# Narrower causal score products, one softmax scale taken out to the head's norm, and one Strassen product added up in PSUM

## The chip, the cores and the metric

The kernel runs on one core of one Trainium2 chip. The metric is the device time of one execution in microseconds; the figure for a kernel is the median of its runs. One more execution is recorded with the hardware profiler: it gives the profile page and the trace from which all rows below come. In them PE is TensorE (matmuls and transposes), PEld its weight loads, DVE is VectorE, ACT is ScalarE, POOL is GpSimd, and SP is the queue that issues most DMAs.

## The reference

One decoder layer over 1024 tokens and 1024 channels, in fp32: RMSNorm; a projection to differential attention (4 heads of two components, dimension 64 each, values 128 wide), sliding-window attention and two gates; a gated merge and a residual; RMSNorm; a gated MLP with a causal convolution of width 3; a residual; a last RMSNorm. The parts that the change touches:

```python
# differential attention, per block of 128 queries
s = einsum(q_blk, k) * scale
logits = where(dist >= 0, s - slopes * dist, NEG_INF)
p = softmax(logits)
a = p[:, :, 0] - lam * p[:, :, 1]
o = einsum(a, v)
o = rmsnorm(o, subln_w) * (1.0 - lam_init)      # over the head's 128 channels, eps 1e-6
...
x = x + (silu(gate) * val) @ w_down             # D_FF = 2816 = 22 blocks of 128
```

## The kernel before

Activations lie with channels on the partitions, so a product of a 128 x 128 weight tile with 512 tokens is one matmul into one PSUM bank. Every fp32 operand is split into a high part (rounded for TensorE, a cast on ScalarE, tiles `wh`, `sh`, `h`) and a low part (a subtraction on VectorE, tiles `wl`, `sl`, the second half of `h`), and a product takes three matmuls: high by high, high by low, low by high. The large products use a seven-product (Strassen-Winograd) scheme on 2 x 2 blocks; the sums of weight blocks that it needs are made by GpSimd in `sum_pair` (L86), which loads a pair of weight tiles `g` and `v`, and are split by `split_pair` (L104).

A tile framework orders the instructions of each engine by priorities and by its own estimates, and sets the waits; each engine, and each DMA queue, then runs its own list strictly in order. Buffers are taken from pools by tag, a fixed number for each; a new tile waits until the last reader of the one whose place it takes is done.

**Attention.** For each head u (4 of them) and each block i of 128 queries, `da_step` (L553) makes the scores of both components against keys 0 to (i+1)*128, rounded up to 256 columns, in cuts of at most 512 (L566, two matmuls for each cut, for the two parts of the keys). VectorE adds the bias and takes the row's extreme (L570), ScalarE takes the exponential and its row sum (L571), VectorE the reciprocal (L572); the second component's is multiplied by -lambda (L574) and applied by ScalarE (L577), and L578 combines both. Transposes to PSUM (L584), a split (L586, L587), and `da_av` (L591) for the product with the values follow. `da_norm` (L601) makes the head's RMSNorm out of column sums on PE (L159), a power -1/2 on GpSimd (`rstd_cols`, L168) and a spread of the result by PE transposes (L174); it is spread over the first steps of the next head. Half-products of the gate projection (`back_half`, L151 to L153, tile `g`) stand between the attention steps and fill PE.

**Down projection.** `down` (L968) treats the 22 blocks of the hidden width in three ranges. Blocks 0 to 5 are plain products in 16 pieces (`self.pieces`, made in `plan`): an output block m (of 8) and a half c (three blocks each); each piece is 2 halves of the tokens by 3 blocks by 3 matmuls, L1016. A bank `pss[m, hf]` holds the sum of both c, and after c = 1 VectorE adds it to the residual `x3` (L1034). `pss[m, 0]` are banks of tag "d", `pss[m, 1]` of tag "y", four of each. In these pieces the h tiles for the later ranges are loaded (`hr`), cast (L748) and made low (L749), and the sums of h blocks for the Strassen part are formed (`sums_h`, L930). Blocks 6 to 13 are the Strassen part. A first loop over m = 0 to 3 makes A11 B11 into a "y" bank and A12 B21 into a "d" bank (`product`, L828 to L830) and adds both to x3 (L1044); a second loop makes the other five products. Blocks 14 to 21 are plain products and the last norm.

Weights for all this come through `next_w` and `ahead` in the order of `self.wsrc`, into three raw buffers (tag "raw"). The pair of weight tiles for the sums of m = 0 (kind "sums") stands before the last two loads of the pieces, and takes two of the three raw buffers until GpSimd's four sums (L97 to L100) are done.

Of the kernel before, what the change touches and what calls it, by code (L numbers as in the profile page):

```python
# [43 lines left out]
class Trunk:  # L44
# [23 lines left out]
    def ahead(self, n):  # L68
        while len(self.wq) < n and self.wsrc and (self.wsrc[0][1] != "pair" or self.uw):
            src, nk, *eng = self.wsrc.pop(0)  # L70
            if nk == "sums":

                self.sums = self.split_pair(*self.sum_pair(src, True), 1, 3)
            elif nk == "rest":
                self.sums["A22"] = self.load_w(src[1][:, 4:8], 4)
                self.wq.append(self.sums)
            elif nk == "pair":
                first, skip = eng or (False, 0)
                self.wq.append(self.split_pair(*self.sum_pair(src, first), skip))
            else:  # L80
                self.wq.append(self.load_w(src, nk, *eng))
        if self.deep and self.wsrc and len(self.wsrc[0]) == 2 and not isinstance(self.wsrc[0][1], str):

            src, nk = self.wsrc[0]
            self.wsrc[0] = src, nk, None, None, self.load_raw(src, nk)

    def sum_pair(self, src, first=False):


        nc = self.nc  # L90
        g = self.tl(self.wp, [P, 2, 4, P], "raw", bufs=RAW)
        nc.sync.dma_start(g.rearrange("p a k c -> p (a k) c"), src[0])
        v = self.tl(self.wp, [P, 2, 4, P], "raw", bufs=RAW) if first else self.tl(self.uw, [P, 2, 4, P], "rv", bufs=2)
        nc.sync.dma_start(v.rearrange("p a k c -> p (a k) c"), src[1])
        sa, sb = (self.tl(self.sfp[0], [P, 2, 4, P], self.sfp[1]) for _ in range(2))
        tt = nc.gpsimd.tensor_tensor
        tt(sa[:, 0], v[:, 0], v[:, 1], ALU.add)  # L97
        tt(sa[:, 1], sa[:, 0], g[:, 0], ALU.subtract)  # L98
        tt(sb[:, 0], g[:, 0], v[:, 0], ALU.subtract)  # L99
        tt(sb[:, 1], g[:, 1], sa[:, 1], ALU.subtract)  # L100
        return g, v, sa, sb
# [116 lines left out]
    def plan(self):  # L218

        self.kind = {m: "q" if m < 4 or 12 <= m < 16 else "k" if m < 8 or m == 16 else "v" if m < 18 else "g" for m in range(34)}  # L220


        self.plain = [0, 4, 8, 18, 20]
        self.pairs = [(1, 5), (9, 2), (6, 10), (3, 7), (11, 12), (13, 16), (17, 14), (15, 19)]
        gates = list(range(21, 34))
        self.back = []
        todo = [(m, hf) for m in gates for hf in range(2)]
        for steps in HALVES:
            self.back.append([[todo.pop(0) for _ in range(n)] for n in steps])
        assert not todo  # L230
        src = [(self.w_in[m], KC) for m in self.plain]
        src += [((self.w_in[a], self.w_in[b]), "pair") for a, b in self.pairs]
        src += [(self.w_in[m], KC) for m in gates]
        src += [(self.w_br[m], KC) for m in range(KC)]
        self.mix_order = [m for k in range(4) for m in (k, k + 4)]
        src += [(self.w_mix[m], KC) for m in self.mix_order]
        src += [((self.w_up[j], self.w_up[j + NF]), "pair") for j in range(NF)]


        n, n2 = N1 // 2, NF - N1 - 8  # L240
        self.pieces = [(m, c) for m0 in (0, 4) for c in range(2) for m in range(m0, m0 + 4)]
        src += [(self.w_dn[m:m + 2, :, n * c:n * c + n, :].rearrange("m p k c -> p m k c"), 2 * n) for m, c in self.pieces[::2]]
        pairs = [(self.w_dn[m, :, N1:N1 + 8, :], self.w_dn[m + 4, :, N1:N1 + 8, :]) for m in range(4)]
        src.insert(len(src) - 2, (pairs[0], "sums"))
        src += [(self.w_dn[m, :, N1:N1 + 8, :], 8) for m in range(4)]
        src += [(pairs[0], "rest")] + [(p, "pair", True, 1) for p in pairs[1:]]
        src += [(self.w_dn[m, :, N1 + 8:, :], n2) for _ in range(2) for m in range(KC)]
        self.wsrc, self.wq, self.deep = src, [], False
# [175 lines left out]
    def attention(self):  # L424
        nc, tc = self.nc, self.tc
        with ExitStack() as ctx:
# [27 lines left out]
            for u in range(6):  # L454
                if st is None:
                    st = self.q_stacks(u), self.kv_stacks(u)
                if u < 4:
                    self.v_parts(u)
                elif u == 4:
                    self.sw_v(self.v32(17))  # L460
                y = self.tl(self.fpool, [P, T], "y", bufs=2) if u < 4 else None
                aT = None
                for i in range(NB):
                    if u < 4:
                        if i % 2 == 0:
                            aT = self.da_at(i // 2)
                        self.da_step(u, i, st, aT)
                        if i % 2 == 1:
                            self.da_av(u, i // 2, aT, y)
                    else:  # L470
                        self.sw_step(u - 4, i, st)
                    for b in self.back[u + 1][i]:
                        self.back_half(*b)
                    self.flush(1)
                    if later:
                        later.pop(0)()
                st = None
                if u < 4:
                    later = self.da_norm(u, y)
# [73 lines left out]
    def da_step(self, h, i, st, aT):  # L553
# [1 line left out]
        q, k = st  # L555
        slope = 4.0 ** -(h + 1)
        w = (i + 1) * P
        wp = (w + 255) // 256 * 256
        pr, rr = [], []
        for c in range(2):  # L560
            sc = self.tl(self.psS, [P, T], "sc")
            qs = q[c][:, i * P:(i + 1) * P]
            for part in range(2):
                for n0 in range(0, wp, H2):
                    n1 = min(n0 + H2, wp)
                    nc.tensor.matmul(sc[:, n0:n1], qs, k[c][part][:, n0:n1], start=part == 0, stop=part == 1)  # L566
            L = self.tl(ap, [P, T], "L", bufs=4)
            s = self.tl(self.st, [P, 4], "sm", bufs=8)
            o = 896 - i * P
            nc.vector.tensor_tensor_reduce(L[:, :w], sc[:, :w], self.bias[:, o:o + w], slope, 3e38, ALU.add, ALU.min, s[:, 0:1])  # L570
            nc.scalar.activation(L[:, :w], L[:, :w], AF.Exp, bias=s[:, 0:1], scale=-1.0, accum_out=s[:, 1:2])  # L571
            nc.vector.reciprocal(s[:, 2:3], s[:, 1:2])  # L572
            if c == 1:
                nc.vector.tensor_tensor(s[:, 2:3], s[:, 2:3], self.neglam, ALU.mult)  # L574
            pr.append(L)
            rr.append(s[:, 2:3])
        nc.scalar.mul(pr[1][:, :w], pr[1][:, :w], rr[1])  # L577
        nc.vector.scalar_tensor_tensor(pr[0][:, :w], pr[0][:, :w], rr[0], pr[1][:, :w], ALU.mult, ALU.add)  # L578
        qo = (i % 2) * P
        for j0 in range(0, i + 1, 4):  # L580
            nj = min(4, i + 1 - j0)
# [19 lines left out]
    def da_norm(self, h, y):  # L601

        nc, ap = self.nc, self.ap
        sqs = []
        for hf in range(2):
            sqs.append(self.tl(ap, [P, H2], "sq", bufs=1))
            nc.scalar.activation(sqs[hf], y[:, hf * H2:(hf + 1) * H2], AF.Square)
# [4 lines left out]

        def sums():
            self.col_sums(ssq, sqs[1:], 4, 4)
            box.append(self.rstd_cols(ssq, 8, P))

        def half(hf):
            ps = self.tl(self.psT, [P, H2], "t")
# [349 lines left out]
    def down(self):  # L968

        nc, tc = self.nc, self.tc  # L970
        with ExitStack() as ctx:
# [31 lines left out]
            for i, (m, c) in enumerate(self.pieces):  # L1003
# [5 lines left out]
                for hf in range(2):  # L1009
                    if c == 0:  # L1010
                        pss[m, hf] = bank(hf)
                    js = range(n * c, n * c + n)
                    for q, j in enumerate(js):
                        h, l = self.hs[hf, j]
                        for p, (v, x) in enumerate(((w[0], h), (w[0], l), (w[1], h))):
                            nc.tensor.matmul(pss[m, hf], v[:, q, :], x, start=c == q == p == 0, stop=c == 1 and q == n - 1 and p == 2)  # L1016
                if i in (2, 8):
                    ms = slice(i // 8 * 4, i // 8 * 4 + 4)
                    nc.sync.dma_start(x3[:, ms], self.x2d[ms].rearrange("m p t -> p m t"))
                for _ in range(n if i < 2 else 1):  # L1020
                    if preps:
# [7 lines left out]
                if i == len(self.pieces) - 1:  # L1029
                    sums.pop(0)()  # L1030
                if c == 1:
                    for hf in range(2):
                        x = col(m, hf)
                        tt(x, x, pss[m, hf], ALU.add)  # L1034
            assert not preps
            ys = []
            for m in range(4):
                wh, wl = self.next_w()
                y, ps = bank(1), bank(0)
                ys.append(y)  # L1040
                self.product(y, (wh[:, 0:4], wl[:, 0:4]), "B11", skip=True)
                self.product(ps, (wh[:, 4:8], wl[:, 4:8]), "B21")
                for p in (y, ps):
                    tt(col(m, 0), col(m, 0), p, ALU.add)  # L1044
                if sums:
                    sums.pop(0)()
# [156 lines left out]
```

## Time and profile before

| | |
|---|---|
| median of 3 runs | 1358.22 us (1357.28 to 1360.21) |
| the profiled execution | 1359.85 us, its span 1358.0 us |
| granted TensorE clock, mean | 0.997 |
| PE busy | 1337.9 us (99% of the span), 6316 matmuls |
| VectorE, ScalarE, GpSimd busy | 1009.0, 623.3, 464.7 us |

A matmul's duration in the trace contains the way through the array, which overlaps with the next one's: where PE is dense, the spacing of starts is what a matmul costs. Rows of the timeline give start, length, engine, line, operation, the tiles written and read, shapes and count; in brackets stands the idle time before it and what ended it. Rows of groups give count, busy time in us, mean duration in ns, and idle time before them. Rows of the view of waits give in total, times, longest.

### The profile page before, as it was taken

Reading aid. Unit: us, or ns where it says so; the run is one execution under the profiler, and the core shown is the slowest. Engines: PE = TensorE matmul, PEld = TensorE weight load, DVE = VectorE, ACT = ScalarE, POOL = GpSimd, SP = SyncE. Lnnn points to the kernel's source line nnn. Section 1 sums busy time; section 2 is a strip of 40 time slices with the busy share of each in tenths; the row PEclk is TensorE's granted clock in tenths of the full one; section 3 lists DMA queues with packets and bytes.
Section 4 is the critical chain, followed back from the end, with each engine's and each line's share of the span. In section 5 each row is a group of like instructions: output and inputs, shape, how many; then the busy total and the mean of one; then the engine's idle time right before and its main releaser. Section 6 shows DMA issues by size and latency. Waiting matters only on the chain.

```text
span 1358.0 us, 17192 instructions
## 1 busy us (share of the span) xinstructions
PE 1337.9 (99%) x6316; PEld 1106.8 (82%) x6316; DVE 1009.0 (74%) x1485; ACT 623.3 (46%) x975; POOL 464.7 (34%) x326
## 2 busy tenths in 40 slices
PE   8999999999999999999999999999999999999997
PEld 6888888788888888888878888888888888788886
DVE  8746774688778966445689889888988898886454
ACT  9432232678776764344354333433343344333343
POOL 0436641000000015642455565556555611231011
PEclk9999999999999999999999999999999999999999
DMA  6334436755654246324522222222222248551342
GB/s 255 140 110 164 145 140 219 205 150 144 171 134 146 79 129 228 140 95 131 162 78 94 78 78 93 69 87 78 93 66 89 85 157 303 190 180 70 92 133 86
DMA packets 62757, 179.50 MB, mean 132 GB/s; under 512 B 6864, under 2 KB 15184, under 8 KB 62672
## 3 DMA queue, kind: packets, MB, share of 16 engines
q1 hardware_dynamic: 50640, 159.93, 36.5%
q10 hardware_dynamic: 12032, 18.46, 3.7%
q8 instruction: 50, 0.82, 0.3%
q14 instruction: 35, 0.29, 0.1%
HBM read 129.61 MB, written 48.76 MB: 131 GB/s over the span
## 4 chain that ended last, share of the span: by engine, by line
PE 61%; DVE 19%; issue 9%; POOL 5%; DMA 2%; ACT 2%; POOLq 0%; SPq 0%; DVEq 0%; ACTq 0%
POOL us L958 5%; PE g L151 5%; PE g L153 5%; PE g L152 5%; PE t L828 4%; PE t L830 4%; PE t L829 4%; PE y L989 3%; PE d L989 3%; PE sc L153 3%; PE sc L152 3%; PE sc L151 3%; DVE wl L113 3%; DVE c L951 3%; PE sc L566 3%
## 5 line engine op out<-in xcount | busy, mean ns | idle before, releaser
L963 ACT ACTIVATE c<-us,vecs 128x1024 f32<-128x1024 f32 x44 | 54.8, 1248 | 163.1 <-POOL us L958 159.6
L958 POOL TENSOR_TENSOR us<-us,rstd 128x1024 f32<-128x1024 f32 x42 | 100.3, 2407 | 53.9 <-DVE wl L132 35.6
L130 ACT CAST wh<-raw 128x1024 fp32r<-128x1024 f32 (+2 forms) x62 | 62.8, 1012 | 110.2 <-PE sc L152 34.9
L111 ACT CAST sh<-sf 128x1024 fp32r<-128x1024 f32 x60 | 62.8, 1050 | 101.3 <-POOL sf L98 62.4
L132 DVE TENSOR_TENSOR wl<-raw,wh 128x1024 fp32r<-128x1024 f32 (+2 forms) x62 | 84.7, 1366 | 31.8 <-ACT wh L130 31.2
L964 DVE SCALAR_TENSOR_TENSOR c<-us,vecs,c 128x1024 f32<-128x1024 f32 x44 | 66.3, 1509 | 51.2 <-ACT c L963 51.2
L97 POOL TENSOR_TENSOR sf<-rv 128x512 f32<-128x512 f32 x29 | 41.9, 1446 | 162.0 <-DMA rv<-in_w_up 63.5
L113 DVE TENSOR_TENSOR sl<-sf,sh 128x1024 fp32r<-128x1024 f32 x60 | 83.7, 1397 | 8.0 <-ACT sh L111 8.0
L718 POOL TENSOR_TENSOR gr<-gr,rstd 128x1024 f32<-128x1024 f32 x16 | 40.3, 2521 | 130.3 <-PE t L670 91.1
L151 PE MATMUL g<-xh,wh 128*128 128x512 f32 x208 | 83.5, 402 | 0.3 <-ACT g L496 0.3
L152 PE MATMUL g<-xl,wh 128*128 128x512 f32 x208 | 83.1, 400 | 0.0
L153 PE MATMUL g<-xh,wl 128*128 128x512 f32 x208 | 82.8, 398 | 0.0
L168 POOL TENSOR_TENSOR rs<-ms,mhalf 128x8 f32<-128x8 f32 (+2 forms) x9 | 14.5, 1609 | 169.6 <-DVE ms L166 163.6
L570 DVE CUSTOM_DVE_ANT_0 L<-sc,bias 128x128 f32<-128x128 f32 (+7 forms) x64 | 47.9, 752 | 22.4 <-PE sc L566 17.3
L99 POOL TENSOR_TENSOR sf<-raw,rv 128x512 f32<-128x512 f32 x29 | 40.4, 1391 | 58.7 <-DVE sl L113 58.7
L965 DVE SCALAR_TENSOR_TENSOR c<-us,vecs,c 128x1024 f32<-128x1024 f32 x44 | 57.2, 1301 | 0.6
L98 POOL TENSOR_TENSOR sf<-sf,raw 128x512 f32<-128x512 f32 x30 | 56.7, 1890 | 1.6
L550 POOL MEMSET aT<- 128x128 f32 x32 | 6.1, 206 | 145.5 <-PE t L597 99.6
L113 DVE TENSOR_TENSOR wl<-raw,wh 128x1024 fp32r<-128x1024 f32 (+1 forms) x34 | 52.5, 1545 | 0.1
L566 PE MATMUL sc<-u,u 128*128 128x512 f32 (+1 forms) x192 | 51.1, 371 | 1.4 <-issue 0.8
L571 ACT ACTIVATE L<-L,sm 128x128 f32<-128x128 f32 (+7 forms) x64 | 49.4, 776 | 6.3 <-DVE sm L570 5.3
L151 PE MATMUL sc<-mh,wh 128*128 128x512 f32 x128 | 49.8, 389 | 0.0
(437 smaller groups left out, 4317.6 us busy)
## 6 DMA issues: line engine op xcount, KB each, us to landing
u<-qd SPq DMA_DIRECT2D x72, 256.0 KB, 6.6
raw<-in_w_down SPq DMA_DIRECT2D x28, 512.0 KB, 3.7
raw<-in_w_in SPq DMA_DIRECT2D x26, 512.0 KB, 4.2
hr<-hd SPq DMA_DIRECT2D x50, 256.0 KB, 5.3
raw<-in_w_up SPq DMA_DIRECT2D x23, 512.0 KB, 3.5
hd<-c SPq DMA_DIRECT2D x22, 512.0 KB, 2.7
rv<-in_w_up SPq DMA_DIRECT2D x21, 512.0 KB, 3.5
gr<-gd SPq DMA_DIRECT2D x16, 512.0 KB, 3.4
```

Of the source, the lines that this page charges most:

```text
L111: nc.scalar.copy(hi, src)
L113: nc.vector.tensor_tensor(lo, src, hi.bitcast(F32), ALU.subtract)
L130: self.hi = nc.scalar.copy(wh, raw)
L132: self.lo = (eng or nc.vector).tensor_tensor(wl, raw, wh.bitcast(F32), ALU.subtract)
L151: nc.tensor.matmul(ps, wh[:, kc + o, :], ah, start=first and n == 0, stop=False)
L152: nc.tensor.matmul(ps, wh[:, kc + o, :], al, start=False, stop=False)
L153: nc.tensor.matmul(ps, wl[:, kc + o, :], ah, start=False, stop=last and n == len(kcs) - 1)
L566: nc.tensor.matmul(sc[:, n0:n1], qs, k[c][part][:, n0:n1], start=part == 0, stop=part == 1)
L958: i = (nc.vector if m % NF == 0 else nc.gpsimd).tensor_tensor(us[:, 2:], us[:, 2:], self.rstd, ALU.mult)
L964: nc.vector.scalar_tensor_tensor(c, us[:, 1:T + 1], cw[1], c, ALU.mult, ALU.add)
L965: nc.vector.scalar_tensor_tensor(c, us[:, 0:T], cw[0], c, ALU.mult, ALU.add)
L989: nc.tensor.matmul(ps, v[:, n, :], x, start=n == i == 0, stop=n == len(js) - 1 and i == 2)
```

## The change

Five edits.

- **Scores of used columns only.** Block i has w = (i+1)*128 keys. Before, the product covered w rounded up to 256. Now it covers w columns, but 256 at i = 0. At w = 640 the scores are laid 128 columns into their two PSUM banks, so that the cuts (384 and 256) fit a bank each.
- **First component's 1/sum in the norm.** With s0 and s1 the row sums of the two exponentials, the kernel now forms E0 - lambda (s0/s1) E1, which is s0 times what it formed before: the reciprocal of s1, then s0 times it times -lambda as one scalar operation, then one combining operation on VectorE. The multiplication on ScalarE and the first reciprocal go. The sums s0 of a head are kept in a 128 x 8 tile, and `da_norm` puts 1/s0 back: the column sums are multiplied by (1/s0) squared ahead of the power, and the result by 1/s0 behind it (on GpSimd).
- **A12 B21 in PSUM.** For m = 0 to 3, `pss[m, 0]` is kept, and A12 B21 of the first loop is added onto it by TensorE; one addition on VectorE then takes both to x3.
- **Order of the pieces.** Output blocks 4 to 7 come first, then 0 to 3; the two loads of x3 follow that.
- **Buffer of the pair's second tile.** For the kind "sums", `v` takes a buffer of tag "sl" of the down projection's pool in place of a raw buffer.

```diff
-                self.sums = self.split_pair(*self.sum_pair(src, True), 1, 3)
+                self.sums = self.split_pair(*self.sum_pair(src, True, "sl"), 1, 3)
...
-    def sum_pair(self, src, first=False):
+    def sum_pair(self, src, first=False, idle=None):
...
-        v = self.tl(self.wp, [P, 2, 4, P], "raw", bufs=RAW) if first else self.tl(self.uw, [P, 2, 4, P], "rv", bufs=2)
+        v = self.tl(self.wp, [P, 2, 4, P], "raw", bufs=RAW) if first and not idle else self.tl(self.uw, [P, 2, 4, P], idle or "rv", bufs=2)
...
-        self.pieces = [(m, c) for m0 in (0, 4) for c in range(2) for m in range(m0, m0 + 4)]
+        self.pieces = [(m, c) for m0 in (4, 0) for c in range(2) for m in range(m0, m0 + 4)]
...
-        wp = (w + 255) // 256 * 256
-        pr, rr = [], []
+        lo = P if w == 640 else 0
+        cuts = ((0, 256),) if i == 0 else ((0, w),) if w <= H2 else ((0, H2 - lo), (H2 - lo, w))
+        pr = []
...
-                for n0 in range(0, wp, H2):
-                    n1 = min(n0 + H2, wp)
-                    nc.tensor.matmul(sc[:, n0:n1], qs, k[c][part][:, n0:n1], start=part == 0, stop=part == 1)
+                for n0, n1 in cuts:
+                    nc.tensor.matmul(sc[:, lo + n0:lo + n1], qs, k[c][part][:, n0:n1], start=part == 0, stop=part == 1)
...
-            nc.scalar.activation(L[:, :w], L[:, :w], AF.Exp, bias=s[:, 0:1], scale=-1.0, accum_out=s[:, 1:2])
-            nc.vector.reciprocal(s[:, 2:3], s[:, 1:2])
-            if c == 1:
-                nc.vector.tensor_tensor(s[:, 2:3], s[:, 2:3], self.neglam, ALU.mult)
+            nc.scalar.activation(L[:, :w], L[:, :w], AF.Exp, bias=s[:, 0:1], scale=-1.0, accum_out=s[:, 1:2] if c else self.s0[:, i:i + 1])
             pr.append(L)
-            rr.append(s[:, 2:3])
-        nc.scalar.mul(pr[1][:, :w], pr[1][:, :w], rr[1])
-        nc.vector.scalar_tensor_tensor(pr[0][:, :w], pr[0][:, :w], rr[0], pr[1][:, :w], ALU.mult, ALU.add)
+
+        nc.vector.reciprocal(s[:, 2:3], s[:, 1:2])
+        nc.vector.tensor_scalar(s[:, 3:4], self.s0[:, i:i + 1], s[:, 2:3], self.neglam, ALU.mult, ALU.mult)
+        nc.vector.scalar_tensor_tensor(pr[0][:, :w], pr[1][:, :w], s[:, 3:4], pr[0][:, :w], ALU.mult, ALU.add)
...
-            box.append(self.rstd_cols(ssq, 8, P))
+            r0, t = (self.tl(self.st, [P, NB], n, bufs=2) for n in ("r0", "r2"))
+            nc.vector.reciprocal(r0, s0)
+            nc.vector.tensor_tensor(t, r0, r0, ALU.mult)
+            nc.vector.tensor_tensor(t, t, ssq[:, :NB], ALU.mult)
+            rs = self.rstd_cols(t, 8, P)
+            nc.gpsimd.tensor_tensor(rs, rs, r0, ALU.mult)
+            box.append(rs)
...
-                            nc.tensor.matmul(pss[m, hf], v[:, q, :], x, start=c == q == p == 0, stop=c == 1 and q == n - 1 and p == 2)
+                            nc.tensor.matmul(pss[m, hf], v[:, q, :], x, start=c == q == p == 0, stop=c == 1 and q == n - 1 and p == 2 and (m > 3 or hf > 0))
...
-                    ms = slice(i // 8 * 4, i // 8 * 4 + 4)
+                    ms = slice(4 - i // 8 * 4, 8 - i // 8 * 4)
...
-                    for hf in range(2):
+                    for hf in range(m < 4, 2):
                         x = col(m, hf)
                         tt(x, x, pss[m, hf], ALU.add)
...
-                y, ps = bank(1), bank(0)
+                y, ps = bank(1), pss[m, 0]
...
-                self.product(ps, (wh[:, 4:8], wl[:, 4:8]), "B21")
+                self.product(ps, (wh[:, 4:8], wl[:, 4:8]), "B21", first=False)
```

More of the change, by code (lines that the diff above doesn't have):

```diff
@@ L464, in attention @@
                     if u < 4:
+                        if i == 0:
+                            self.s0 = self.tl(self.st, [P, NB], 's0', bufs=2)
                         if i % 2 == 0:
@@ L569, in da_step @@
             o = 896 - i * P
-            nc.vector.tensor_tensor_reduce(L[:, :w], sc[:, :w], self.bias[:, o:o + w], slope, 3e38, ALU.add, ALU.min, s[:, 0:1])
-            nc.scalar.activation(L[:, :w], L[:, :w], AF.Exp, bias=s[:, 0:1], scale=-1.0, accum_out=s[:, 1:2])
-            nc.vector.reciprocal(s[:, 2:3], s[:, 1:2])
-            if c == 1:
-                nc.vector.tensor_tensor(s[:, 2:3], s[:, 2:3], self.neglam, ALU.mult)
+            nc.vector.tensor_tensor_reduce(L[:, :w], sc[:, lo:lo + w], self.bias[:, o:o + w], slope, 3e38, ALU.add, ALU.min, s[:, 0:1])
+            nc.scalar.activation(L[:, :w], L[:, :w], AF.Exp, bias=s[:, 0:1], scale=-1.0, accum_out=s[:, 1:2] if c else self.s0[:, i:i + 1])
             pr.append(L)
-            rr.append(s[:, 2:3])
-        nc.scalar.mul(pr[1][:, :w], pr[1][:, :w], rr[1])
-        nc.vector.scalar_tensor_tensor(pr[0][:, :w], pr[0][:, :w], rr[0], pr[1][:, :w], ALU.mult, ALU.add)
+        nc.vector.reciprocal(s[:, 2:3], s[:, 1:2])
+        nc.vector.tensor_scalar(s[:, 3:4], self.s0[:, i:i + 1], s[:, 2:3], self.neglam, ALU.mult, ALU.mult)
+        nc.vector.scalar_tensor_tensor(pr[0][:, :w], pr[1][:, :w], s[:, 3:4], pr[0][:, :w], ALU.mult, ALU.add)
         qo = (i % 2) * P
@@ L603, in da_norm @@
         nc, ap = self.nc, self.ap
-        sqs = []
+        sqs, s0 = [], self.s0
         for hf in range(2):
```

## Prediction, made before the changed kernel ran

> **What bounds the kernel now.** I read the page's first two parts, then the windows by stage, then the PE timeline wherever a window is short of full, and last the queues that feed that place.
>
> ```profile
> span 1358.0 us, 17192 instructions
> PE 1337.9 (99%) x6316; PEld 1106.8 (82%) x6316; DVE 1009.0 (74%) x1485; ACT 623.3 (46%) x975; POOL 464.7 (34%) x326
> ```
>
> ```profile
> 240.00:480.00 240.00, 238.73 (x1417) 1.00 0.52 144
> ...
> 1180.00:1200.00 20.00, 18.27 (x73) 0.91 0.65 215
> ```
>
> The windows' columns are stretch, length, PE busy (count), granted clock, DMA share, GB/s. TensorE has work 99% of the span; in attention (240 to 480 us) it is idle for 1.27 of 240 us. So time comes off in two ways only: columns that PE need not stream, or one of its few holes. The one hole that this change touches lies at 1180 to 1200, where PE is 1.73 us short and the clock falls to 0.91. Work taken from ScalarE or VectorE elsewhere buys nothing by itself.
>
> **The score products.** PE's pace is the spacing of starts, not a matmul's duration. The chain of waits gives it for 256 and for 512 columns, the PE timeline for 512-column scores among other attention work:
>
> ```profile
> 392.54 1.92 PE sc L650 x16
> 1257.75 5.44 PE d L989 x24
> ```
>
> ```profile
> 264.08 0.86 PE L566 MATMUL sc<-u,u 128*128 128x512 f32 x3
> 264.79 0.27 PE L597 MATMUL t<-aT,v 128*128 128x256 f32 x1
> ```
>
> 256 columns cost 1.92/16 = 0.120 us, 512 cost 5.44/24 = 0.227, and in attention (264.79 - 264.08)/3 = 0.237. The new cuts leave i = 0, 1, 3, 5 and 7 alone; at i = 2, 4 and 6 one 512-wide product becomes 384 wide: 3 steps x 2 components x 2 parts x 4 heads = 48 matmuls. No row shows 384 columns. On the line between 256 and 512 it takes 0.227 - 0.107/2 = 0.1735 us, 0.0535 less, so 48 x 0.0535 = **2.6 us**, all on PE's path. (With 0.237, 2.8.) The bounds: as dear as 512 columns, 0; as cheap as 256, 48 x 0.107 = 5.1. I take the line, because each of the 48 sits between two measured widths of the same instruction. It could also be dearer than 512: 128-column transposes start 0.109 us apart,
>
> ```profile
> 266.56 0.71 PE L584 MATMUL t<-ident,L 128*128 128x128 f32 x5
> 267.02 0.48 PE L151 MATMUL g<-xh,wh 128*128 128x512 f32 x1
> ```
>
> where five start within 0.46 us, the last spaced short. At 0.109 per 128 columns, 384 would cost 0.327, or 48 x 0.100 = 4.8 us more than now; I give that little weight, since those are plain fp32 transposes.
>
> The Trainium skill, TensorE: Matmul & The Clock Gate, section Back-to-back issue gap, says that in a stream of weight load and matmul the spacing is set by both, 81 ns at 128 columns and 131 at 512. By that slope 128 columns are worth 17 ns and the edit 0.8 us. The trace disagrees with the level (0.227 at 512), and its own slope between 256 and 512 is the one used above.
>
> **Softmax and norm.** Off ScalarE go 32 multiplications, off VectorE 32 reciprocals; a scalar product takes the place of the one with -lambda.
>
> ```profile
> L577 ACT ACTIVATE L<-L,sm 128x128 f32<-128x128 f32 (+7 forms) x32 | 24.3, 775 | 2.7 <-DVE sm L574 2.3 <-DVE sm L572 0.3
> L572 DVE RECIPROCAL sm<-sm 128x1 f32<-128x1 f32 x64 | 9.6, 157 | 6.2 <-ACT L L571 6.0
> ```
>
> That is 24.3 us of ScalarE and 5.0 of VectorE, beside a PE that idles 1.27 us in the whole stage, with gate products between the softmax steps. I book 0. The order of the changed program has the same attention work on PE, with fewer gate matmuls between some steps, so a wait may come or go; I bound it at 1.3 gained (all idle) and 2 lost. Each head's norm gets a reciprocal and two 128x8 products on VectorE (0.16 each, like L572) and one 128x8 product on GpSimd, ahead of the transposes at L174:
>
> ```profile
> 287.98 1.65 POOL L168 TENSOR_TENSOR rs<-ms,mhalf 128x8 f32<-128x8 f32 x1 [3.24 <-DVE sm L572]
> ```
>
> ```profile
> 293.35 0.60 PE L174 MATMUL t<-ident,rs 128*128 128x128 f32 x4
> ```
>
> rs is ready at 289.63, its reader starts at 293.35: 3.7 us of cover. At worst the GpSimd product costs as much as this power, 1.65, and VectorE 0.3 behind the sums. It stays hidden; without cover it would be 4 x 2 = 8 us.
>
> **The down projection's hole.** PE's rows there:
>
> ```profile
> 1182.72 0.39 PE L830 MATMUL d<-h,wl 128*128 128x512 f32 x1
> 1184.23 0.50 PE L828 MATMUL y<-h,wh 128*128 128x512 f32 x1 [1.12 <-ACT wh L130]
> 1184.56 0.40 PE L829 MATMUL y<-h,wh 128*128 128x512 f32 x1
> 1185.57 0.50 PE L830 MATMUL y<-h,wl 128*128 128x512 f32 x1 [0.61 <-DVE wl L132]
> ...
> 1186.75 0.63 PE L828 MATMUL y<-h,wh 128*128 128x512 f32 x1
> ...
> 1189.74 0.43 PE L829 MATMUL d<-h,wh 128*128 128x512 f32 x1
> 1190.01 0.39 PE L830 MATMUL d<-h,wl 128*128 128x512 f32 x1
> ```
>
> From 1182.72 to 1190.01 there are 15 steps (the rows left out counted), 3.40 us at 0.227; it takes 7.29. The hole costs **3.89 us**: 1.28 and 0.78 waiting for the second weight tile (m = 1) of the A11 / A12 loop, and the rest, 1.83, mostly because the seven spacings from 1186.75 to 1189.74 are 0.427, nearly half pace. Why it was late:
>
> ```profile
> ACT h L748 <- DVE hr L936: 6.4, 1, 6.4
> ```
>
> ```profile
> 1170.01 1.23 DVE L113 TENSOR_TENSOR sl<-c,sh 128x1024 fp32r<-128x1024 f32 x1 [2.27 <-ACT sh L111]
> 1171.15 0.68 DVE L1034 TENSOR_TENSOR x<-x,d 128x512 f32<-128x512 f32 x1
> ...
> 1183.70 0.68 DVE L1034 TENSOR_TENSOR x<-x,y 128x512 f32<-128x512 f32 x1
> 1184.30 1.21 DVE L132 TENSOR_TENSOR wl<-raw,wh 128x1024 fp32r<-128x1024 f32 x1
> ```
>
> VectorE works without a pause from 1171.15, 21 operations deep (an add lets the next start after 0.60 us, a low part like sl after 1.14), before that tile's low part, and ScalarE's cast of the high part stands behind two h casts that wait for VectorE. The change takes four of the adds away (A12 B21 lands in the same bank) and moves others: in the changed program's order 14 operations stand there, 13 of 0.60 and one low part of 1.14.
>
> Against this the pair's second tile v goes to a "sl" buffer whose memory still holds parts of hidden tiles; its load now waits for PE's last use of them, in piece 11 (before, it had a raw buffer that came free earlier), and the casts of the sums stand ahead of the first A11 weight on ScalarE. Worked forward:
>
> ```profile
> 1159.60 0.39 PE L1016 MATMUL y<-sl,wl 128*128 128x512 f32 x1
> ```
>
> ```profile
> 1163.07 1.62 POOL L98 TENSOR_TENSOR c<-c,raw 128x512 f32<-128x512 f32 x1
> 1164.66 2.00 POOL L99 TENSOR_TENSOR c<-raw,raw 128x512 f32<-128x512 f32 x1
> 1166.62 2.27 POOL L100 TENSOR_TENSOR c<-raw,c 128x512 f32<-128x512 f32 x1
> ```
>
> ```profile
> 1160.06 9.67 SPq L120 DMA_DIRECT2D raw<-in_w_down  x4
> ```
>
> ```profile
> raw<-in_w_down SPq DMA_DIRECT2D x28, 512.0 KB, 3.7
> ```
>
> ```profile
> 1168.92 1.05 ACT L111 CAST sh<-c 128x1024 fp32r<-128x1024 f32 x1 [3.14 <-POOL c L100]
> ```
>
> ```profile
> 1177.51 0.39 PE L828 MATMUL y<-h,wh 128*128 128x512 f32 x1
> ```
>
> PE lets v's place go at 1159.99; the load of the first A11 weight leaves SP ahead of it, at 1160.06, so v leaves about 1160.5 and lands at 1164.2. GpSimd's four sums: three take 5.82 here, with a first like L98 7.4, so 1171.6. The sh cast ends at 1172.7, its low part (1.23) at 1173.9, and 14 operations later (13 x 0.60 + 1.14) VectorE starts the m = 1 low part at 1182.8, done at 1184.0. PE starts m = 0 at 1177.51 (its own low part is done at 1175.7, needed at 1177.96), m = 1 24 x 0.227 later at 1182.96, and needs that low part at 1183.41: late by 0.6. With v landing in 3.2 to 4.9 us and sums of 6.1 to 7.4 it is on time or late by up to 1.7. I book 0.7 left, with no half pace, so **3.2 us** gained (2.2 with 1.7 left and full pace; 0.4 if the 1.83 of half pace stay too; 3.9 at most). Queued behind v on SP are the m = 1 and m = 2 weights, wanted 20 us later, and h loads for the same sums. x3's two loads trade halves, at the same places.
>
> The Trainium skill, TensorE: Matmul & The Clock Gate, Part 1 (the HAM clock gate), has half clock after an idle window of some 3.4 us. Here two waits of 2.06 us together, within 2.6, were enough; by the page the half pace would not be there at all, and the hole worth 2.06. The measurement decides.
>
> **The sum.** 2.6 + 0 + 3.2 = 5.8 us. The profiled execution took 1359.85 us (its span 1358.0 and 1.9 around it), so 1354.05 for its like. It stood 1.63 above the median of the three runs, 1358.22; on the level of that median I predict 1352.4.
>
> **Rivals.**
> 1. The forecast, with the score saving on the line and the hole nearly shut: 1350.5 to 1354.5 by itself. Chance 0.55.
> 2. The hole stays half open: late by 1.7, and the clock falls again. Then 2.6 + 0.4 = 3.0, 1355.2. For it: ScalarE and VectorE now wait for the sums ahead of the A11 weights. Against: 7 fewer operations in the queue. 0.16.
> 3. The 384-wide product costs what 512 costs, so that part doesn't do what it says: 3.2 gained by the hole alone, 1355.0. For it: each matmul has its own weight load (6316 of each). Against: 256 columns do run at 0.120. 0.09.
> 4. More than forecast: the softmax chain, shorter by a ScalarE multiplication of 0.78, closes attention's idle time, and the hole shuts fully: 2.8 + 1.3 + 3.9 = 8.0, 1350.2 or below. 0.08.
> 5. Slower: v lands late. If it takes 6.6 us, as the stacks' loads do, and the sums 9.65 (1159.24 to 1168.89, the waiting first one included), the low part of the sums ends at 1179.0 instead of 1173.9. Then m = 0 waits to 1180.8 instead of 1177.96 (2.8), m = 1 another 2.9, and each pays 1.8 of half pace: 9.3 against 3.9. Net 5.4 - 2.6 = 2.8 slower, 1361.0. It decides from an end of the sums' low part 4 us past 1173.3. For it: rows as long exist.
>
> ```profile
> u<-qd SPq DMA_DIRECT2D x72, 256.0 KB, 6.6
> 1159.24 3.75 POOL L97 TENSOR_TENSOR c<-raw 128x512 f32<-128x512 f32 x1 [6.56 <-DVE c L951]
> ```
>
> Against: loads of this very source take 3.7. With dearer 384-wide products (1361.0 if both gains were lost to them) 0.12.
>
> **How the numbers follow.** About 0.2%, 2.7 us, is what a measurement here can tell from no change. Faster by more than that, below 1355.5: cases 1 and 4 and half of 2 and 3 (1355.0 and 1355.2 lie near the edge), 0.75. Within: the other half and mild forms of 5, 0.15. Slower: 0.10. The range takes case 4 at its low end, 1349.0, and on the high end cases 2 and 3 together (0.4 left of gain, 1357.8): 1349.0 to 1357.8.
>
> **What would show it.** 48 score rows of 384 columns spaced 0.17; L577's row gone with PE's idle in attention as before, within 1 to 2 us; the window after the down pieces at clock 1.00 with at most one wait, under 1 us, at the second A11 weight; v's load near 1160 of the old clock. Wrong, if PE waits over 2 us there, if spacings of 0.43 return, or if attention has grown.

## The result, and the profile after

The changed kernel takes 1362.24 us (median of 8 runs, 1361.71 to 1363.84) where the kernel before takes 1358.40 in the same comparison (8 runs, 1356.93 to 1360.21): a ratio of 1.003, 95% interval 1.0019 to 1.0041. It is slower, by some 4 us, where 6 us of gain were forecast. The profiled execution took 1363.84 us.

The first lines of the changed kernel's page, and its windows for attention and for the place of the hole in the down-projection (columns as in the prediction, with PE, PEld, DVE, ACT and POOL in turn):

```profile
span 1362.1 us, 17126 instructions
...
PE 1344.8 (99%) x6316; PEld 1108.5 (81%) x6316; DVE 1014.3 (74%) x1461; ACT 604.3 (44%) x943; POOL 464.2 (34%) x330
```

```profile
240.00:480.00 240.00, 238.40 (x1429) 204.49 (x1428) 195.08 (x596) 156.48 (x400) 12.68 (x35) 1.00 0.53 147
1180.00:1200.00 20.00, 19.53 (x87) 15.85 (x86) 18.01 (x27) 7.01 (x10) 0.00 (x0) 1.00 0.69 225
```

Both places that the change edits are better. The hole is down from 1.73 us to 0.47 and the clock is full, and ScalarE is relieved by 19 us. PE is nevertheless busy 6.9 us longer with the same 6316 matmuls, 48 of which became narrower. A busy time that grows with less to stream says that matmuls have become slower. Where the time went, the starts of PE's matmuls show; the five columns run from the start of the trace to the last matmul:

| us | up to the first gate product | attention | merge and mix | hidden stage | down-projection and end |
|---|---|---|---|---|---|
| before | 219.8 | 289.4 | 173.8 | 429.2 | 239.6 |
| after | 223.7 | 286.4 | 174.8 | 432.5 | 238.5 |

Attention won 3.0 us and the down-projection 1.1. What was lost stands in three stages of which the change does not touch a line: 3.9, 1.0 and 3.3 us. The groups of PE's matmuls between 60 and 200 us, before and after (columns: count, then busy us and mean ns of one):

```profile
L828 PE MATMUL t<-xh,wh 128*128 128x512 f32 x56 | 21.8, 389 | 0.0
L829 PE MATMUL t<-xl,wh 128*128 128x512 f32 x56 | 21.8, 389 | 0.0
L830 PE MATMUL t<-xh,wl 128*128 128x512 f32 x56 | 21.8, 389 | 0.0
```

```profile
L835 PE MATMUL t<-xh,wh 128*128 128x512 f32 x56 | 22.1, 394 | 0.0
...
L837 PE MATMUL t<-xh,wl 128*128 128x512 f32 x56 | 22.0, 392 | 0.0
...
L836 PE MATMUL t<-xl,wh 128*128 128x512 f32 x56 | 21.7, 388 | 0.0
```

The three lines that are L828 to L830 before are L835 to L837 after. Their matmuls last 5, 3 and -1 ns longer, and the windows of 140 us, PE full and the clock at 1.00 in both, hold 619 matmuls before and 613 after:

```profile
60.00:200.00 140.00, 140.00 (x619) 115.99 (x618) 90.03 (x88) 41.07 (x48) 72.67 (x41) 1.00 0.41 147
```

```profile
60.00:200.00 140.00, 140.00 (x613) 114.89 (x612) 91.97 (x87) 40.93 (x48) 71.90 (x40) 1.00 0.43 153
```

In spacings that is 231.7, 229.2 and 225.8 ns for the three rows after, in their order, where all were 226 to 227. Added up over all 512-wide matmuls of the trace that are spaced under 260 ns, pace above 226.7 ns costs 3.4 us before and 15.9 after. 8.6 us of the latter lie in the hidden stage, where what spacings over 260 ns (mostly waits) add shrank from 6.8 to 2.3 us: a slower PE probably finds more of its operands ready.

The stage after attention holds the clue. In the merge and the mix, lines L151 to L153 run the same shapes; three groups between 512 and 685 us before, and six after:

```profile
L151 PE MATMUL sc<-mh,wh 128*128 128x512 f32 x128 | 49.8, 389 | 0.0
L152 PE MATMUL sc<-ml,wh 128*128 128x512 f32 x128 | 49.8, 389 | 0.0
L153 PE MATMUL sc<-mh,wl 128*128 128x512 f32 x128 | 49.8, 389 | 0.0
```

```profile
L151 PE MATMUL sc<-mh,wh 128*128 128x512 f32 x128 | 50.4, 394 | 0.0
L153 PE MATMUL sc<-mh,wl 128*128 128x512 f32 x128 | 50.2, 392 | 0.0
L152 PE MATMUL sc<-ml,wh 128*128 128x512 f32 x128 | 49.7, 388 | 0.0
L151 PE MATMUL g<-yh,wh 128*128 128x512 f32 x64 | 24.9, 389 | 0.0
L152 PE MATMUL g<-yl,wh 128*128 128x512 f32 x64 | 24.9, 389 | 0.0
L153 PE MATMUL g<-yh,wl 128*128 128x512 f32 x64 | 24.9, 389 | 0.0
```

After, the groups with `mh` and `ml` as the moving operand (the one that is streamed past the weights) have changed, those with `yh` and `yl` have 389 ns as before. In the built kernel the three tiles that the norm's edit adds to the pool `st` (`s0`, `r0`, `r2`: two buffers of 32 bytes per partition each, 192 in all) push up by 192 bytes every pool that is allocated after it from the left end of SBUF (the on-chip memory that both operands are read from): `raw` from 9216 to 9408, `wh` from 21504 to 21696. Pools allocated from the right end stay (`xh0` at 163328). Before, both operands of every 512-wide matmul begin at a multiple of 256 bytes. After, `wh`, `yh` and `yl` are 192 off and `mh`, `ml` and `xh` 0 off: in this stage slow where weight and moving operand differ, at pace where they agree. In the hidden stage the rule does not hold matmul by matmul: `B_0h` with `wh`, both 192 off, is spaced 233 ns in the mean, and `B_3h` with `wh`, the last block of the same products, 226.7. One of these products starts right behind matmuls whose offsets differ, so a slow pace seems to carry over for a while; no run isolates that.

### The profile page after: what moved, and what is told of

Its sections match the earlier page's. It is cut to its first block, busy times and chain, and to the rows that moved or that the text cites. A ratio compares the mean times of both kernels' runs of the same rounds, so it can differ in the third digit from the quotient of the medians.

```text
span 1362.1 us, 17126 instructions
## 1 busy us (share of the span) xinstructions
PE 1344.8 (99%) x6316; PEld 1108.5 (81%) x6316; DVE 1014.3 (74%) x1461; ACT 604.3 (44%) x943; POOL 464.2 (34%) x330
## 4 chain that ended last, share of the span: by engine, by line
PE 95%; DVE 3%; issue 1%; DMA 0%; ACT 0%; POOLq 0%; SPq 0%; POOL 0%; ACTq 0%
PE t L837 14%; PE t L835 14%; PE t L836 14%; PE g L151 5%; PE g L153 5%; PE g L152 5%; PE d L996 3%; PE sc L151 3%; PE y L996 3%; PE sc L153 3%; PE sc L152 3%; PE sc L569 3%; PE d L1023 2%; PE y L1023 2%; PE t L585 1%; PE sc L657 1%
## 5 line engine op out<-in xcount | busy, mean ns | idle before, releaser
L151 PE MATMUL g<-xh,wh 128*128 128x512 f32 x208 | 83.5, 401 | 0.2 <-ACT g L498 0.2
L153 PE MATMUL g<-xh,wl 128*128 128x512 f32 x208 | 83.1, 399 | 0.0
L151 PE MATMUL sc<-mh,wh 128*128 128x512 f32 x128 | 50.4, 394 | 0.0
L153 PE MATMUL sc<-mh,wl 128*128 128x512 f32 x128 | 50.2, 392 | 0.0
```

The lines of the kernel that those rows point to most:

```text
L151: nc.tensor.matmul(ps, wh[:, kc + o, :], ah, start=first and n == 0, stop=False)
L153: nc.tensor.matmul(ps, wl[:, kc + o, :], ah, start=False, stop=last and n == len(kcs) - 1)
```

## The experiments

All ratios are against runs of the kernel before on the same chip, with 95% intervals. A difference in us is the ratio's share of 1358 us; differences of the medians are up to 1 us away from it. The theory (A in the expectations) is placement.

**Placement alone.** The computation and the order of PE's matmuls are those of the kernel before:

```diff
             self.st = ctx.enter_context(tc.tile_pool(name="st", bufs=4))
+            pw = ctx.enter_context(tc.tile_pool(name="pad_w", bufs=1))
+            pw.tile([P, 48], F32, name="pad_w_t")      # 192 bytes, never used
```

> The kernel before, its computation untouched, with one unused tile of 192 bytes per partition between the small-tile pool and the weight pool, so that everything allocated on the left after it lies 192 bytes higher, as in the changed kernel. Theory A (placement: the matmuls of untouched stages pace at 229 to 233 ns instead of 227 because their operands moved by 192 bytes): 0 to 240 us loses 2.1 to 4.2 us, merge and mix 1.1, the hidden stage 3.3, the down-projection 2.2, attention nothing, so 1366 to 1369 us. Rival B (the loss comes from the edits themselves, their new waits and their new order): no change, 1358.4 us, pace 227 ns. Rival C (the loss is only the clock's phase at the start, drawn anew in every program): anywhere within 2 us of 1358.4, pace 227 ns.

1365.47 us, ratio 1.0057 (1.0044 to 1.0070): an unused tile costs 7.7 us, a little less than the 1366 to 1369 us expected, and rivals B and C are out. Its groups between 60 and 200 us have the changed kernel's durations (394, 392 and 388 ns, on other lines):

```profile
L831 PE MATMUL t<-xl,wh 128*128 128x512 f32 x56 | 22.1, 394 | 0.0
...
L830 PE MATMUL t<-xh,wh 128*128 128x512 f32 x56 | 22.0, 392 | 0.0
...
L832 PE MATMUL t<-xh,wl 128*128 128x512 f32 x56 | 21.7, 388 | 0.0
```

**The change with its weights where they were.** The kernel reserves 480 bytes at each end of SBUF; the left reserve gives 192 of them back, so that the constants and small tiles move down by 192 and the weights lie where they lay:

```diff
-LPAD, RPAD = 480, 480
+LPAD, RPAD = 288, 480
```

> The changed kernel with the left pad at 288 instead of 480 bytes: the weight pool and all left pools after it lie where they lay before the change (the constants and small tiles below them move down by 192 bytes). Theory A: the 4.2 us lost ahead of attention, 1.1 in merge and mix, 3.3 in the hidden stage and 2.2 at the end come back: 1362.2 - 10.6 = 1351.6 us, or 1353.5 if the half-pace matmuls of the first 15 us have another cause; L835 to L837 pace at 227 ns. Rival B: 1362 us as the changed kernel. Rival C: within 2 us of 1362.

1352.74 us, ratio 0.9966 (0.9954 to 0.9978). The change is then worth 4.6 us, it beats both kernels, and its groups are back. The identity that the transposes stream moved with the constants; transposes start 109 ns apart (median) here and before:

```profile
L836 PE MATMUL t<-xl,wh 128*128 128x512 f32 x56 | 21.8, 389 | 0.0
L835 PE MATMUL t<-xh,wh 128*128 128x512 f32 x56 | 21.8, 389 | 0.0
L837 PE MATMUL t<-xh,wl 128*128 128x512 f32 x56 | 21.8, 389 | 0.0
```

**Both sides moved.** The changed kernel, left pools as it has them, right pools up by 192 bytes too:

```diff
-LPAD, RPAD = 480, 480
+LPAD, RPAD = 480, 288
```

> The changed kernel with the right pad at 288 instead of 480 bytes: the pools on the right (the moving operands of the projections among them) also move up by 192 bytes, so that left and right tiles have the same offset of 192 within 512 bytes. Theory A in the form that only the offset between the two operands counts: 1352 to 1354 us, pace 227 ns. Theory A in the form that tiles must start at multiples of 512 bytes: no better than the changed kernel, 1362 to 1368 us, pace 229 to 234 ns. Rivals B and C: 1362 us.

1354.20 us, ratio 0.9978 (0.9968 to 0.9988), which agrees with the run before it within the intervals, and the mix is at pace:

```profile
L151 PE MATMUL sc<-mh,wh 128*128 128x512 f32 x128 | 49.8, 389 | 0.0
L153 PE MATMUL sc<-mh,wl 128*128 128x512 f32 x128 | 49.8, 389 | 0.0
L152 PE MATMUL sc<-ml,wh 128*128 128x512 f32 x128 | 49.8, 389 | 0.0
```

So it is not the multiple of 256 (or 512) that counts, but that both operands have the same offset.

**The period.** The unused tile of the first experiment with 64 floats (256 bytes), 32 (128) and 16 (64).

> The kernel before with an unused tile of 256 bytes per partition ahead of the weight pool: the left pools move by half of 512 bytes. Theory A with a period of 256 bytes (or one shorter): 1358.4 us, pace 227 ns. Theory A with a period of 512 bytes or more: 1362 to 1369 us, pace 229 ns and more, as with 192 bytes. Rivals B and C: 1358.4 us.

> The kernel before with an unused tile of 128 bytes per partition ahead of the weight pool. Theory A with a period of 128 bytes: no change, pace 227 ns. Theory A with a period of 256 bytes: slower by 5 to 10 us, pace 229 ns and more, as with 192 bytes (1.0057). Theory A with a period of 128 bytes and 192 bytes being half a period off is then shown by the first outcome, and the second leaves 256.

> The kernel before with an unused tile of 64 bytes per partition ahead of the weight pool. Theory A, symmetric form (only the distance to the nearest multiple of 256 bytes counts): as with 192 bytes, 1.0057 or 7.7 us on, matmuls at 226 to 233 ns. If instead the loss grows with the offset in bytes (128: 13.4 us): under 1.0057. Theory A is refuted by 1357 us and 227 ns.

256 bytes: 1356.88 us, ratio 0.9998 (0.9989 to 1.0007), nothing. 128 bytes: 1370.85, 1.0099 (1.0085 to 1.0113). 64 bytes: 1368.57, 1.0084 (1.0071 to 1.0096). One row between 60 and 200 us of each, in that order:

```profile
L831 PE MATMUL t<-xl,wh 128*128 128x512 f32 x56 | 21.8, 389 | 0.0
```

```profile
L831 PE MATMUL t<-xl,wh 128*128 128x512 f32 x56 | 22.1, 394 | 0.0
```

```profile
L831 PE MATMUL t<-xl,wh 128*128 128x512 f32 x56 | 22.1, 396 | 0.0
```

The offset repeats after 256 bytes. At 128 the loss, 13.4 us, is more than the 5 to 10 expected. Both forms expected of 64 are wrong: it costs more than 192, so neither the distance to the nearest multiple of 256 counts, nor does the loss grow with the offset. The traces say what does. In each kernel whose left pools are moved by 64, 128 or 192 bytes, some 512-wide products have only their weights moved and others only their moving tile. Sorted by the addresses of the built kernels, the mean spacings (those under 260 ns, to a 512-wide neighbour) go by the weights' offset less the moving tile's, modulo 256: for 64 it is 233.2 ns in the kernel with 64 unused bytes and 233.3 in the changed kernel, for 192 it is 229.6 and 229.7 in the same two, for 128 it is 232.7 and 232.8 in the two directions, and 227.2 where it is 0 in all products. So the sign of the difference counts, and 64 and 192 are not alike. What in the memory makes it so, no run shows.

**The three parts alone**, each with the weights at their old offset; the diffs are those of the change, and the norm's part, which adds the small tiles, has `LPAD, RPAD = 288, 480`.

> The kernel before with the narrower score products alone; no small tile is added, so every tile lies where it lay. The prediction's first step: 2.6 us off (bounds 0 and 5.1), with all of it inside the attention heads; theory D (attention is not a pure queue of matmuls, and part of what PE no longer multiplies turns into waiting for the scores' softmax): 0.5 to 1.5 us off. Theory A says only that the pace of the other stages stays at 227 ns.

> The kernel before with the norm's part alone (1/sum of the first component applied in the head's norm, ScalarE's pass at L577 gone), the left pad at 288 bytes so that the three new small tiles don't move the weight pools. The prediction's second step: 0 (bounds 1.3 us off, 2 us on). Theory D: 0.5 to 2 us off, since a shorter softmax chain takes waits off the attention steps. Without the pad it would be 7 us slower by theory A.

> The kernel before with the down-projection's part alone (order of the pieces, the idle buffer for the sum, A12 B21 accumulated in PSUM), every tile where it lay. The prediction's third step: 3.2 us off, the hole at 1182 to 1190 us shrinking from 3.9 us to under 1. Theory D says nothing of it. If the sum of the three parts is to give the 4.6 us by which the changed kernel with its weights at their old offset beat the kernel before (0.9966 of 1358.2), one of the three steps gives some 1.2 us less than predicted.

Scores alone: 1360.77 us, 1.0029 (1.0018 to 1.0040), slower by 3.9. Norm alone: 1360.48, 1.0025 (1.0016 to 1.0034), slower by 3.4. Down alone: 1356.00, 0.9990 (0.9981 to 0.9999), faster by 1.4. The sum, 5.9 slower, is on the other side of the 4.6 gained by all three together, and none of the theories said that. Neither the 2.6 expected of the scores nor the 3.2 of the down-projection came, and theory D, with small gains for scores and norm, is out too. Stage by stage, as in the first table:

| us | first | attention | merge and mix | hidden | down and end |
|---|---|---|---|---|---|
| change, old offset | 219.5 | 286.0 | 173.9 | 428.7 | 236.9 |
| scores alone | 219.4 | 292.4 | 173.9 | 428.7 | 237.6 |
| norm alone | 219.9 | 291.2 | 173.9 | 428.1 | 237.7 |
| down alone | 218.9 | 288.5 | 173.8 | 429.0 | 236.8 |

In the profiled executions the scores alone grew in attention by 3.0 us and the norm alone by 1.8, and no other stage of them grew by more than 0.1; three kernels with the order of before in attention (192 and 256 unused bytes, down alone) have 289.6, 288.6 and 288.5 there. The rest of the norm's 3.4 us its one trace does not show: that execution stood 1.5 us under its median. PE's waits in attention (240 to 512 us) with the scores alone, and the window of 380 to 420 us of the same kernel and of the kernel before:

```profile
PE t L585 <- DVE sw L656: 1.8, 1, 1.8
PE sc L567 <- issue: 0.9, 1, 0.9
PE t L671 <- DVE v L638: 0.9, 1, 0.9
PE g L151 <- ACT g L496: 0.8, 1, 0.8
PE sc L651 <- DVE sw L654: 0.8, 2, 0.5
```

```profile
380.00:420.00 40.00, 35.72 (x232) 31.96 (x231) 34.82 (x130) 31.96 (x86) 2.08 (x3) 0.96 0.46 116
```

```profile
380.00:420.00 40.00, 40.00 (x254) 34.59 (x254) 30.95 (x107) 27.40 (x70) 1.84 (x2) 1.00 0.56 147
```

Here the last differential head hands over to the window heads. Both kernels have 624 gate matmuls to put between attention's, and the framework's scheduler lays them out anew for each kernel. With the scores alone it has used more of them early: 37 start between 380 and 420 us, where the kernel before has 72. PE has too little to fill its waits there, is idle for 4.3 us, and the clock is down to 0.96. With the norm alone PE waits elsewhere, 1.3 us for a load of the next window head's stacks and 0.8 for ScalarE.

**The order of the gate matmuls.** The scores alone, laid out differently:

```diff
-                        self.da_step(u, i, st, aT)
+                        with self.tc.high_priority(60):
+                            self.da_step(u, i, st, aT)
```

> The narrower score products alone, as in the run of scores alone, but with a higher scheduling priority for the attention steps of the four differential heads, so that the scheduler lays the gate projection's matmuls differently between them: the longest stretch of PE's order without a gate matmul falls from 19336 columns to 16904 (10248 in the kernel before). Theory E (scores alone lost 3.6 us because the scheduler spent the gate matmuls early and left the hand-over to the window heads bare, with 4.6 us of waits at 393 to 412 us): a part of those waits goes, 1356.5 to 1359.5 us beside 1357.1 for the kernel before. Rival F (narrow score products cost time whatever stands between them): 1360.8 us again.

1357.53 us, ratio 1.0004 (0.9994 to 1.0013): 3.4 us back, with the same score products. Its window:

```profile
380.00:420.00 40.00, 38.60 (x246) 32.81 (x245) 34.90 (x127) 32.10 (x85) 1.84 (x2) 1.00 0.47 113
```

Idle there is 1.4 us instead of 4.3, and attention takes 288.6 us. 54 gate matmuls start in it. The priority moves more than the gate matmuls, so this supports the theory (E) without isolating it; rival F, that narrow products cost time in any order, is out.

**Scores and norm together**, without the down-projection's part, left pad at 288.

> Score and norm parts together, without the down-projection's part, the left pad at 288 bytes so that the weights keep their offset. Its matmul order in attention is that of the changed kernel (longest stretch without a gate matmul 11784 columns). Theory E (what counts is the order that the scheduler draws for the combination): the 4.6 us of the changed kernel at the old offset less the 1.4 us of the down-projection's part, 3.2 us off: 1353.9 us beside 1357.1. Rival G (the parts add up): 3.6 + 3.3 us on, 1364 us.

1353.38 us, ratio 0.9972 (0.9961 to 0.9983): 3.8 us gained by two parts that each lose over 3 alone, near the 1353.9 of theory E and far from the 1364 of rival G. Its attention takes 285.4 us, and this is all that PE waits for in it:

```profile
PE g L151 <- ACT g L498: 0.2, 1, 0.2
PE t L677 <- DVE L L670: 0.2, 1, 0.2
```

That the parts don't add up is shown; that the drawn order is the reason is shown in part for the scores, and only argued for the norm. The longest stretch without a gate matmul, by which the expectations measure the order, does not explain the norm: in its built kernel that is 11272 columns, fewer than the 11784 of the fast combination.

## Why the prediction was wrong

**The step that failed is "Softmax and norm ... I book 0", bounded at 2 us lost.** It counted the instructions of the edit and the cover of its chain, and not that its three small tiles lie ahead of the weight pools. Their place costs 7.7 us by the unused tile, or 8.7 by the changed kernel with and without the offset (1.003 less 0.9966, from two comparisons). The opening was too narrow in the same way: "time comes off in two ways only", columns and holes, took the 0.227 us of untouched stages as given. Without this loss 1358.40 x 0.9966 = 1353.8 would have been within the range, though with other terms than those booked, as the next paragraphs show.

**The score products: price right, yield not theirs alone.** The changed kernel's rows for one stretch:

```profile
294.81 0.82 PE L569 MATMUL sc<-u,u 128*128 128x384 f32 x4
295.47 0.55 PE L585 MATMUL t<-ident,L 128*128 128x128 f32 x3
```

(295.47 - 294.81)/4 = 0.165, the last spaced short; the median spacing of all 48 is 0.176, against 0.1735 booked. That gives 48 x 0.051 = 2.4 us. Rival 3 (384 at the price of 512) and the dearer end are out. But in the kernel of that edit alone other waits took the gain and more, so "all on PE's path" held for the columns and not for the time.

**The norm's chain** stayed hidden: the changed kernel's waits in attention are the two shown last and one of 1.0 us at its start. The gain that rival 4 saw there came, for scores and norm together: 3.4 to 4.0 us less attention, where 2.6 were booked.

**The hole: mechanism right, size wrong.** The changed kernel there:

```profile
1188.53 0.39 PE L835 MATMUL y<-h,wh 128*128 128x512 f32 x1
1188.75 0.39 PE L836 MATMUL y<-h,wh 128*128 128x512 f32 x1
1189.61 0.50 PE L837 MATMUL y<-h,wl 128*128 128x512 f32 x1 [0.47 <-DVE wl L132]
1189.95 0.39 PE L835 MATMUL y<-h,wh 128*128 128x512 f32 x1
```

The one wait left costs 1189.61 - 1188.75 - 0.227 = 0.63 us; 0.7 was booked, at that tile. The sums came as worked out too:

```profile
1169.18 1.76 POOL L97 TENSOR_TENSOR c<-sl 128x512 f32<-128x512 f32 x1 [13.73 <-DVE h L756]
...
1174.42 1.63 POOL L100 TENSOR_TENSOR c<-raw,c 128x512 f32<-128x512 f32 x1
```

The stage begins 5.2 us later than before, so they end at 1176.05 - 5.2 = 1170.9 of the old clock, where 1171.6 was reckoned. Rival 5, v late, named nearly the measured time (1361.0) for a cause that did not happen: that was luck. What was mis-sized is the 3.2: it took in 1.83 of half pace, and the part alone gives 1.4 (0.1 to 2.6 by its interval), which is near 2.06 of waits less 0.63. The kernel before with 256 unused bytes shows why. Its waits between 1170 and 1260 us, and its window of that place:

```profile
PE y L830 <- ACT wh L130: 1.1, 1, 1.1
PE y L832 <- DVE wl L132: 1.1, 2, 0.6
PE y L830 <- DVE x L1057: 0.2, 1, 0.2
```

```profile
1178.00:1198.00 20.00, 18.27 (x79) 14.39 (x79) 19.86 (x31) 9.04 (x14) 0.00 (x0) 1.00 0.65 214
```

The first row and one of the second are the same two waits as before (1.28 and 0.78 in spacings; the second row's other one ends nearly 8 us earlier). PE is busy for the same 18.27 us, yet the clock is 1.00 and not 0.91, with 79 matmuls in place of 73. The pair comes back at nearly this length in two more traces: with the scores at higher priority (1.06 and 0.77) no half pace follows, with scores and norm together (1.07 and 0.78) seven spacings of 0.427 do. So the half pace behind such waits is not a fixed price of theirs; it looks like a draw of the execution, though no kernel was traced twice. That agrees with the Trainium skill, TensorE: Matmul & The Clock Gate, Part 1 (the HAM clock gate), which calls the gate's window free-running. The hole at 2.06, which the prediction set aside with "the measurement decides", came nearer; that measurement was one execution.

The same holds for the start. The first 16 us of before, of after, and of the kernel before with 192 unused bytes:

```profile
0.00:16.00 16.00, 9.38 (x29) 6.78 (x30) 9.59 (x12) 12.72 (x14) 0.78 (x8) 1.00 0.90 347
```

```profile
0.00:16.00 16.00, 9.18 (x20) 5.65 (x21) 8.81 (x11) 11.94 (x14) 0.78 (x8) 1.00 0.89 343
```

```profile
0.00:16.00 16.00, 9.12 (x31) 6.58 (x32) 9.34 (x11) 12.46 (x14) 0.78 (x8) 1.00 0.90 348
```

The changed kernel gets 20 matmuls into them, the others 29 and 31, although the third has its weights 192 bytes off as well. By the starts in the traces, spacings of 0.427 us and more give way to full pace at 12.3, 15.4 and 10.8 us (the clock column, 1.00 in all three, does not show it). Of the 3.9 us lost ahead of attention in the profiled execution, 1.9 are pace above 226.7 ns, the offset; the other 2 go with this later change to full pace, and that execution stood 1.6 us above its median.

**The list of what would show it** was met point by point: 384-wide rows at 0.17 to 0.18 (40 of the 48), L577's multiplication gone, one wait under 1 us at clock 1.00, no spacing of 0.43 there, v's load at 1160.3 of the old clock, attention not grown. All of it watched the edited places. A line on the mean duration of an untouched group, 389 ns, would have caught the loss.

## What to carry to other kernels

A change is also what it allocates: before pricing instructions, compare the addresses of the tiles that fill TensorE's stream, and if a new small tile moves a pool, add filler or take it from a reserve so that weights and moving operands keep the same offset within 256 bytes. Read a suspected loss first in the groups of stages that nobody edited. And where a scheduler lays out filler work, an edit's gain in a dense stage belongs to the order drawn for that combination: try edits together and apart, at fixed placement.

## What the runs showed of the hardware

- Where weight and moving tile of all 512-wide matmuls have the same offset within 256 bytes, these are spaced 227.2 ns in the mean (226.7 in dense stages). Where the weights lie 64, 128 or 192 bytes above the moving tile, modulo 256, it is 233, 233 and 230 ns. With the left pools 64, 128 and 192 bytes up, the whole kernel takes 1.0084, 1.0099 and 1.0057 of its time; 256 bytes cost nothing, and moving both sides by 192 takes the loss away.
- Two waits of together 1.8 to 2.1 us, ending 1.3 us apart, were followed by seven spacings at half pace (0.427 us) in two profiled executions and by none in two others, of kernels that are alike there.
- 384 columns are spaced 0.176 us (median), near the line between 0.120 for 256 and 0.227 for 512, which gives 0.1735.
